# Layer B's output blocks and attention steps in another order

## The chip, the cores and the metric

The kernel runs on one core of a Trainium2 chip. The metric is the device time of one execution in microseconds (us), lower is better. The kernel before has a median of 1008.8 us over three runs (1007.71 to 1010.31).

Five engines matter: TensorE (PE in the profile) multiplies matrices, VectorE (DVE) and ScalarE (ACT) work on elements, GpSimd (POOL) issues some of the transfers, and SyncE (SP) issues the transfers of the weights. Each has its own list of instructions.

## The reference, cut to what matters

A trunk of two layers over 256 tokens of width 2048: layer A is a Mamba-2 mixer, layer B is attention over a window of 128 keys with one sink per head. Both end in a LayerNorm of `alpha * x + mixer(x)`. Layer B, which the change touches, computes:

```python
proj = x @ w_in                                # 2048 -> [q 2048 | gate 2048]
q = rope(proj[..., :2048] + q_bias)            # 32 heads of 64; 4 key groups of 8 heads
s = q . k * 64 ** -0.5                         # window of 128: masked elsewhere
m = max(max(s), sink);  p = exp(s - m)
p = p / (sum(p) + exp(sink - m))
o = (p @ v) * silu(gate)
x = layernorm(alpha * x + o @ w_out)
```

Keys and values are computed once, for 4 key groups, each shared by 8 query heads. The kernel handles one key group (512 columns of q, of the gate and of the input of `w_out`) at a time.

## The kernel before, in words

**Units of weights.** All weights stream through SBUF in units of 128 x 2048 numbers. `load_unit` (L120) fetches a unit in two halves of 512 KB from SyncE's queue into one of five raw buffers `wr`, and then splits each half into a high part `wh` (ScalarE, L133) and a low part `wl` (VectorE, L134), so that three matmuls of rounded operands give the product (`wh` and `wl` have four buffers each). `next_unit` (L179) keeps two units ahead of the one that TensorE works on.

**Layer B's blocks.** The work is a list of twelve blocks of four units each, `B_ORDER` (L39). For key group j:

- `q_block(j)` (L790): queries. Four units add into two PSUM tiles (one per half h of the 256 tokens), 24 matmuls of 512 columns a unit (L751 to L753). Then VectorE takes both tiles out of PSUM with the bias (L801), applies the rotary part (L739 to L744) and transposes 32 x 32 squares (`zq`, L806). GpSimd writes the result to DRAM (`qd`, L847) and reads it back turned (`qr`, L813); ScalarE scales it into `qT` (L817).
- `gate_block(j)` (L829): the gate, 48 matmuls of 256 columns a unit (L195 to L197), one PSUM tile a unit, then ScalarE and VectorE (L838, L839).
- `attend(j, h)` (L853): scores of one half (TensorE, L864), mask (L872, L873, L877), maximum (L881), exponentials (ScalarE, L887), division (L892). Then `turn_p` transposes into `z` (L898) and writes it to DRAM (`pd`, L847), `load_p` reads it back as `pT` (L905), `mask_p` makes a second, masked copy `pm` (L912, for h = 1 alone), and `pv` multiplies with the values (TensorE, L922) and with the gate, and splits the result into `oH` and `oL` (L929, L938, L939).
- an output block `("o", j)`: `out_unit` (L249) multiplies `oH`, `oL` with the units of `w_out`, 24 matmuls of 512 columns a unit (L255 to L257) into two PSUM tiles, one for each half; VectorE adds each to the residual `xr` (L264; L260 in the first block).

All matmuls of the blocks share four PSUM tiles `mm` (L81), the scores and values share another four, `ax` (L84). `z`, `zq`, `qr`, `p`, `pT` and `pm` share five buffers with the tag `pb`.

**Steps.** One unit is one step. After each unit `tick` (L204) counts down a list, `pending`; `later(n, fn)` (L201) puts a function on it that runs n steps on. So the attention of a key group is spread over the units of the blocks that follow its queries. Counted from the step T at which `q_block(j)` ends, before the change:

| what | step, j = 0 to 2 | step, j = 3 |
| --- | --- | --- |
| `load_q` (both halves) | T + 1 | T + 1 |
| `scale_q` (both halves) | T + 3 | T + 3 |
| `attend(j, 0)` | T + 4 | T + 4 |
| `attend(j, 1)` | T + 7 | T + 5 |
| `turn_p`, `load_p` of h = 0 | T + 6, T + 7 | T + 6, T + 7 |
| `turn_p`, `load_p` of h = 1 | T + 9, T + 10 | T + 7, T + 8 |
| `pv` of h = 0, of h = 1 | T + 10, T + 13 | T + 10, T + 11 |

With step 1 as the first unit of `("q", 0)`, the query blocks end at steps 4, 12, 20 and 32, and the output blocks start at steps 25, 33, 41 and 45.

**What sets the order.** The Python program is written in this order, and a planner then makes each engine's list from it when the kernel is built. It follows an estimate of its own of when each instruction's inputs are there; of those that are ready by that estimate, the one that was written earlier goes first. A step is thus an instruction's rank, not a fixed place: an instruction that the planner believes ready can stand ahead of ones written earlier whose inputs it expects later. What comes out is a fixed list for each engine, with waits; on the chip an instruction whose input is late holds up what stands behind it on its engine.

Of the kernel before, what the change touches and what calls it, by code (L numbers as in the profile page):

```python
# [35 lines left out]
BLOCKS = list(range(10))  # L36
BLOCKS0 = [6, 7, 8, 9, 0, 1, 2, 3, 4, 5]
CB_AT, ZT_AT, LD_AT, XD_AT, Y_AT, NSM = 4, 5, 6, 8, 9, 3
B_ORDER = [("q", 0), ("g", 0), ("q", 1), ("g", 1), ("q", 2), ("g", 2), ("o", 0), ("q", 3),  # L39
           ("o", 1), ("g", 3), ("o", 2), ("o", 3)]  # L40
ALPHA = (2.0 * 2) ** 0.25
NEG = -1.0e30
# [15 lines left out]
def trunk(ctx: ExitStack, tc: tile.TileContext, A: dict, out: bass.AP, dbg=None):  # L58
# [17 lines left out]
    def nm(s):  # L76
        uid[0] += 1
        return f"{s}_{uid[0]}"

    def mm_tile():  # L80
        return mm_ps.tile([P, 512], F32, tag="mm", name=nm("mm"), bufs=4)  # L81
# [89 lines left out]
    broken = set()  # L171
    for what, j in B_ORDER:
        if what == "g":
# [5 lines left out]
    def next_unit():  # L179
        if not units:  # L180
            units.extend(load_first())
            nc.sync.dma_start(pc[:], A["pc"])
        while len(units) < min(used[0] + 1 + AHEAD, len(srcs)):
            if len(units) == 5:
                nc.sync.dma_start(cc[:], A["cc"])
            if len(units) in (8, 9):
                i = len(units) - 8
                nc.sync.dma_start(xr[:, i, :], A["xk"][:, i, :])
                nc.scalar.activation(xr[:, i, :], xr[:, i, :], AF.Copy, scale=ALPHA)
            units.append(load_unit(srcs[len(units)], BROKEN if len(units) in broken else [WHOLE, WHOLE]))  # L190
        used[0] += 1
        return units[used[0] - 1]
# [8 lines left out]
    def later(n, fn):  # L201
        pending.append([n, fn])

    def tick():  # L204
        ready = []
        for it in list(pending):
            it[0] -= 1
            if it[0] <= 0:
                pending.remove(it)
                ready.append(it[1])  # L210
        for fn in ready:
            fn()
# [36 lines left out]
    def out_unit(aH, aL, h, u, nb, first, rms=None):  # L249

        ps = mm_tile()
        hs = slice(h * P, (h + 1) * P)
        for k in range(4):
            ks = slice(k * 512, (k + 1) * 512)
            nc.tensor.matmul(ps[:], aH[:, k, hs], u.h[:, ks], start=k == 0, stop=False)  # L255
            nc.tensor.matmul(ps[:], aL[:, k, hs], u.h[:, ks], start=False, stop=False)  # L256
            nc.tensor.matmul(ps[:], aH[:, k, hs], u.l[:, ks], start=False, stop=k == 3)  # L257
        v = xr[:, h, nb * 512 : (nb + 1) * 512]
        if first:
            nc.vector.scalar_tensor_tensor(v, v, ALPHA, ps[:], ALU.mult, ALU.add)  # L260
        elif rms is not None:
            nc.vector.scalar_tensor_tensor(v, ps[:], rms[:, h : h + 1], v, ALU.mult, ALU.add)
        else:
            nc.vector.tensor_tensor(v, v, ps[:], ALU.add)  # L264
# [462 lines left out]
    def bias_row(src):  # L727
        t = bp.tile([P, 512], F32, tag="bias", name=nm("bias"), bufs=2)
        nc.gpsimd.dma_start(t[:], src.partition_broadcast(P))
        return t  # L730

    def rope(v, h, n):

        c = cs[:, h : h + 1, :].to_broadcast([P, n, 8])
        s = sn[:, h : h + 1, :].to_broadcast([P, n, 8])
        t = bp.tile([P, 4, 8, 8], F32, tag="rt", name=nm("rt"), bufs=1)
        x1, x2 = v[:, :, 0:8], v[:, :, 8:16]
        a, b, d, e = [t[:, i, :n, :] for i in range(4)]
        nc.vector.tensor_tensor(a, x1, c, ALU.mult)  # L739
        nc.vector.tensor_tensor(b, x2, s, ALU.mult)  # L740
        nc.vector.tensor_tensor(d, x2, c, ALU.mult)
        nc.vector.tensor_tensor(e, x1, s, ALU.mult)
        nc.vector.tensor_tensor(x1, a, b, ALU.subtract)
        nc.vector.tensor_tensor(x2, d, e, ALU.add)  # L744

    def x_stat(ps, h, u, ui):
        for k in range(4):
            kk = ui * 4 + k
            ks = slice(k * 512, (k + 1) * 512)
            hs = slice(h * P, (h + 1) * P)  # L750
            nc.tensor.matmul(ps[:], x1H[:, kk, hs], u.h[:, ks], start=kk == 0, stop=False)  # L751
            nc.tensor.matmul(ps[:], x1L[:, kk, hs], u.h[:, ks], start=False, stop=False)  # L752
            nc.tensor.matmul(ps[:], x1H[:, kk, hs], u.l[:, ks], start=False, stop=kk == KT - 1)  # L753
# [36 lines left out]
    def q_block(j):  # L790
        pss = [mm_tile(), mm_tile()]
        qb = bias_row(A["qb"][j * 512 : (j + 1) * 512])
        for ui in range(4):
            u = next_unit()
            for h in range(2):
                x_stat(pss[h], h, u, ui)
            tick()
        for h in range(2):
            qt = bp.tile([P, 8, 64], F32, tag="qt", name=nm("qt"), bufs=2)
            qf = qt[:].rearrange("p a d -> p (a d)")  # L800
            nc.vector.tensor_tensor(qf, pss[h][:], qb[:], ALU.add)  # L801
            rope(qt[:], h, 8)

            def turn_q(h=h, qf=qf):
                z = bp.tile([P, 1024], F32, tag="pb", name=nm("zq"), bufs=5)[:, :512]
                nc.vector.transpose(  # L806
                    z.rearrange("p (c a t) -> p a c t", c=4, a=4), qf.rearrange("p (a c d) -> p a c d", a=4, c=4)
                )
                d = to_dram(z, 128, "qd")

                def load_q():
                    t = bp.tile([P, 8, 4, 32], F32, tag="pb", name=nm("qr"), bufs=5)[:, :4]
                    nc.gpsimd.dma_start(t.rearrange("p b a t -> p b (a t)"), d[:].rearrange("b p f -> p b f"))  # L813

                    def scale_q():
                        q2 = bp.tile([P, 4, P], F32, tag="qT", name=nm("qT"), bufs=2)
                        nc.scalar.activation(  # L817
                            q2[:].rearrange("p a (b t) -> p a b t", b=4), t.rearrange("p b a t -> p a b t"),
                            AF.Copy, scale=0.125,
                        )  # L820
                        qT[j, h] = q2

                    later(2, scale_q)

                later(1, load_q)

            turn_q()

    def gate_block(j):  # L829
        t = bp.tile([P, 4, S], F32, tag="sg", name=nm("sg"), bufs=2)  # L830
        sg[j] = t
        for p_ in range(4):
            u = next_unit()
            ps = mm_tile()
            for k in range(KT):
                mac(ps[:, :S], u.tile(0, k), u.tile(1, k), x1H[:, k, :], x1L[:, k, :], k == 0, k == KT - 1)
            tick()
            nc.scalar.activation(t[:, p_, :], ps[:, :S], AF.Tanh, scale=0.5)  # L838
            nc.vector.scalar_tensor_tensor(  # L839
                t[:, p_, :], t[:, p_, :], 1.0, ps[:, :S], ALU.add, ALU.mult  # L840
            )

    def to_dram(z, n, name):

        t = dram.tile([4, P, n], F32, tag=name, name=nm(name), bufs=2)
        for a in range(4):
            nc.gpsimd.dma_start(  # L847
                t[a, :, :].rearrange("(b t) f -> t b f", b=4),
                z[32 * a : 32 * a + 32, :].rearrange("p (b f) -> p b f", b=4),
            )  # L850
        return t

    def attend(j, h):  # L853
# [84 lines left out]
            nc.scalar.activation(oH[:, :, hs], o[:], AF.Copy)  # L938
            nc.vector.tensor_tensor(oL[:, :, hs], o[:], oH[:, :, hs].bitcast(F32), ALU.subtract)  # L939

        last = j == 3
        later(2, turn_p)
        later(3, load_p)
        later(5, mask_p)
        later(6, pv)
        if h == 0:
            later(1 if last else 3, lambda: attend(j, 1))

    for what, j in B_ORDER[:-1]:
        if what == "q":  # L950
            q_block(j)
            later(4, lambda j=j: attend(j, 0))
        elif what == "g":
            gate_block(j)
        else:
            for nb in range(4):
                u = next_unit()
                for h in range(2):
                    out_unit(*os_[j], h, u, nb, j == 0)
                tick()  # L960
# [140 lines left out]
```

## Time and profile before

| | |
| --- | --- |
| median of three runs | 1008.8 us (1007.71 to 1010.31) |
| the profiled execution | 1005.46 us |
| its span (first to last instruction) | 1003.6 us |
| PE busy | 983.6 us (98%) |
| DVE busy | 778.8 us (78%) |
| ACT busy | 559.3 us (56%) |
| POOL busy | 137.9 us (14%) |
| mean granted TensorE clock | 0.994 |
| first scores of layer B (L864) | 739.9 us from the span's start |
| last scores | 925.9 us |
| last values (L922) | 964.2 us |

PE's busy time counts an instruction from its start to a modelled end; matmuls overlap, so the pace of a stretch is read from the starts. The granted clock is a share of full speed. In a timeline or a group of instructions the bracket or the last column tells how long the engine stood idle before the instruction, and what ended that idle time.

### The profile page before, as it was taken

What the parts mean: (1) busy time and instruction counts of PE and PEld (TensorE: products, weight loads), DVE (VectorE), ACT (ScalarE), POOL (GpSimd) and SP (SyncE); (2) the same over time, 40 slices, a digit from 0 to 9 for tenths busy, and PEclk for the clock granted to TensorE, in tenths of its full rate; (3) what the DMA queues carried; (4) which work ended last, traced back from release to release, by engine and by line L of the source; (5) the groups of instructions that cost most, each with busy time, mean ns of one, the idle gap of its engine ahead of it and who ended that gap; (6) DMA issues with size and microseconds to landing.
All of it is one profiled execution on the core that took longest, in us unless ns stands there. A gap on an engine that the chain in (4) does not pass through costs nothing.

```text
span 1003.6 us, 17483 instructions
## 1 busy us (share of the span) xinstructions
PE 983.6 (98%) x6844; PEld 886.8 (88%) x6844; DVE 778.8 (78%) x1116; ACT 559.3 (56%) x928; POOL 137.9 (14%) x192
## 2 busy tenths in 40 slices
PE   7999999999999999999999999999999999998997
PEld 7999999999998998999999999877898888777965
DVE  6869997876797796796787687799658596966876
ACT  6585757637655665664664664445455464633632
POOL 0000303004003001200300300301204031110202
PEclk9999999999999999999999999999999999998998
DMA  8787686586677667667658458646757667566552
GB/s 314 273 276 258 199 277 230 164 286 168 210 232 222 216 203 244 205 190 254 200 174 278 143 195 272 231 133 224 237 184 243 229 214 248 191 226 209 185 216 85
DMA packets 69875, 219.24 MB, mean 218 GB/s; under 512 B 8144, under 2 KB 19680, under 8 KB 69024
## 3 DMA queue, kind: packets, MB, share of 16 engines
q1 hardware_dynamic: 64080, 199.48, 61.0%
q0 software_dynamic: 5424, 18.12, 5.2%
q8 instruction: 54, 0.88, 0.4%
q10 hardware_dynamic: 288, 0.52, 0.1%
q14 instruction: 29, 0.24, 0.1%
HBM read 205.90 MB, written 12.19 MB: 217 GB/s over the span
## 4 chain that ended last, share of the span: by engine, by line
PE 78%; DVE 7%; DMA 6%; ACT 4%; issue 3%; POOL 1%; SPq 0%; DVEq 0%; ACTq 0%; POOLq 0%
PE mm L195 15%; PE mm L196 15%; PE mm L197 15%; PE mm L255 7%; PE mm L256 6%; PE mm L257 6%; PE mm L751 3%; PE mm L752 3%; PE mm L753 3%; DVE wl L134 2%; PE ax L510 2%; ACT wh L133 2%; DMA wr<-in_wa 1%; PE ax L864 1%; PE ax L922 1%
## 5 line engine op out<-in xcount | busy, mean ns | idle before, releaser
L134 DVE TENSOR_TENSOR wl<-wr,wh 128x1024 fp32r<-128x1024 f32 (+2 forms) x342 | 397.4, 1180 | 114.1 <-ACT wh L133 112.7
L133 ACT ACTIVATE wh<-wr 128x1024 fp32r<-128x1024 f32 (+2 forms) x342 | 338.0, 1011 | 190.9 <-PE mm L196 68.1
L195 PE MATMUL mm<-xH,wh 128*128 128x256 f32 x1296 | 360.5, 278 | 6.2 <-ACT wh L153 5.5
L197 PE MATMUL mm<-xH,wl 128*128 128x256 f32 x1296 | 359.6, 278 | 1.9 <-DVE wl L134 1.9
L196 PE MATMUL mm<-xL,wh 128*128 128x256 f32 x1296 | 360.0, 278 | 0.0
L195 PEld LDWEIGHTS mm<-xH,wh 128*128 128x128 f32 x1296 | 244.5, 189 | 8.1 <-ACT wh L153 5.8
L197 PEld LDWEIGHTS mm<-xH,wl 128*128 128x128 f32 x1296 | 244.3, 189 | 2.6 <-DVE wl L134 2.6
L196 PEld LDWEIGHTS mm<-xL,wh 128*128 128x128 f32 x1296 | 244.5, 189 | 1.1
L526 POOL TENSOR_TENSOR yz<-yz,z 128x256 f32<-128x256 f32 x32 | 33.7, 1063 | 524.3 <-DVE yz L521 482.9
L255 PE MATMUL mm<-wh,yH 128*128 128x512 f32 x256 | 101.3, 396 | 0.0
L256 PE MATMUL mm<-wh,yL 128*128 128x512 f32 x256 | 99.9, 390 | 0.0
L257 PE MATMUL mm<-wl,yH 128*128 128x512 f32 x256 | 99.7, 389 | 0.0
L195 PE MATMUL mm<-x1H,wh 128*128 128x256 f32 x256 | 72.6, 284 | 3.0 <-DVE xr L264 3.0
L196 PE MATMUL mm<-x1L,wh 128*128 128x256 f32 x256 | 72.0, 281 | 0.0
L197 PE MATMUL mm<-x1H,wl 128*128 128x256 f32 x256 | 72.0, 281 | 0.0
L364 DVE SCALAR_TENSOR_TENSOR cv<-mm,pc,cv 128x255 f32<-128x255 f32 x144 | 68.7, 477 | 2.0 <-ACT cv L362 0.6
L751 PE MATMUL mm<-wh,x1H 128*128 128x512 f32 x160 | 63.5, 397 | 0.0
L753 PE MATMUL mm<-wl,x1H 128*128 128x512 f32 x160 | 62.7, 392 | 0.2 <-DVE wl L134 0.2
L752 PE MATMUL mm<-wh,x1L 128*128 128x512 f32 x160 | 62.6, 391 | 0.2 <-DVE x1L L715 0.2
L255 PEld LDWEIGHTS mm<-wh,yH 128*128 128x128 f32 x256 | 48.1, 188 | 10.7 <-DVE z L434 1.0
L257 PEld LDWEIGHTS mm<-wl,yH 128*128 128x128 f32 x256 | 48.1, 188 | 10.2
L256 PEld LDWEIGHTS mm<-wh,yL 128*128 128x128 f32 x256 | 48.1, 188 | 8.9
(188 smaller groups left out, 1317.0 us busy)
## 6 DMA issues: line engine op xcount, KB each, us to landing
wr<-in_wa SPq DMA_DIRECT2D x158, 512.0 KB, 5.3
wr<-in_wo SPq DMA_DIRECT2D x64, 512.0 KB, 4.9
wr<-in_wq SPq DMA_DIRECT2D x32, 512.0 KB, 5.0
wr<-in_wg SPq DMA_DIRECT2D x32, 512.0 KB, 5.4
wr<-in_wb SPq DMA_DIRECT2D x32, 512.0 KB, 6.5
rb<-rscr SPq DMA_DIRECT2D x16, 512.0 KB, 5.4
el<-rscr SPq DMA_DIRECT2D x16, 256.0 KB, 4.9
wr<-in_wkv SPq DMA_DIRECT2D x8, 512.0 KB, 5.0
```

Of the source, the lines that this page charges most:

```text
L133: nc.scalar.activation(h[:, sl], raw, AF.Copy)
L134: nc.vector.tensor_tensor(l[:, sl], raw, h[:, sl].bitcast(F32), ALU.subtract)
L195: nc.tensor.matmul(ps, ah, bh, start=first, stop=False)
L196: nc.tensor.matmul(ps, ah, bl, start=False, stop=False)
L197: nc.tensor.matmul(ps, al, bh, start=False, stop=last)
L255: nc.tensor.matmul(ps[:], aH[:, k, hs], u.h[:, ks], start=k == 0, stop=False)
L256: nc.tensor.matmul(ps[:], aL[:, k, hs], u.h[:, ks], start=False, stop=False)
L257: nc.tensor.matmul(ps[:], aH[:, k, hs], u.l[:, ks], start=False, stop=k == 3)
L364: nc.vector.scalar_tensor_tensor(a[:, sft:], ps[:, : S - sft], w(3 - sft), a[:, sft:], ALU.mult, ALU.add)
L751: nc.tensor.matmul(ps[:], x1H[:, kk, hs], u.h[:, ks], start=kk == 0, stop=False)
L752: nc.tensor.matmul(ps[:], x1L[:, kk, hs], u.h[:, ks], start=False, stop=False)
L753: nc.tensor.matmul(ps[:], x1H[:, kk, hs], u.l[:, ks], start=False, stop=kk == KT - 1)
```

## The change

Three things are altered. The block `("q", 3)` moves ahead of `("o", 0)`. `scale_q` comes four steps after `load_q` and not two, and the scores of h = 0 six steps after the end of the query block and not four, with those of h = 1 one step later for every key group (before: three steps for the first three, one for the last). And `mask_p` and `pv` come one step later after their scores (6 and 7, not 5 and 6).

```diff
-B_ORDER = [("q", 0), ("g", 0), ("q", 1), ("g", 1), ("q", 2), ("g", 2), ("o", 0), ("q", 3),
+B_ORDER = [("q", 0), ("g", 0), ("q", 1), ("g", 1), ("q", 2), ("g", 2), ("q", 3), ("o", 0),
            ("o", 1), ("g", 3), ("o", 2), ("o", 3)]
...
-                    later(2, scale_q)
+                    later(4, scale_q)
...
-        last = j == 3
         later(2, turn_p)
         later(3, load_p)
-        later(5, mask_p)
-        later(6, pv)
+        later(6, mask_p)
+        later(7, pv)
         if h == 0:
-            later(1 if last else 3, lambda: attend(j, 1))
+            later(1, lambda: attend(j, 1))
 
     for what, j in B_ORDER[:-1]:
         if what == "q":
             q_block(j)
-            later(4, lambda j=j: attend(j, 0))
+            later(6, lambda j=j: attend(j, 0))
```

After it, for every j: `scale_q` at T + 5, the scores at T + 6 and T + 7, `turn_p` at T + 8 and T + 9, `load_p` at T + 9 and T + 10, `mask_p` of h = 1 at T + 13, `pv` at T + 13 and T + 14. The query blocks end at steps 4, 12, 20 and 28; the first output block starts at step 29 and no longer at 25, the others at 33, 41 and 45 as before. No instruction is added or left out, and the streams of weights differ in order alone.

## The prediction

> **What bounds the kernel now.** The first view is the profile's page: TensorE is busy for nearly the whole span.
>
> ```profile
> PE 983.6 (98%) x6844; PEld 886.8 (88%) x6844; DVE 778.8 (78%) x1116; ACT 559.3 (56%) x928; POOL 137.9 (14%) x192
> ```
>
> No matmul is added or removed, so the change can move only time in which TensorE stands still or runs slowly inside layer B. The second view, what TensorE waited for from 640 us to the end, lists all of it (total us, times, longest):
>
> ```profile
> PE mm L195 <- DVE xr L264: 3.0, 1, 3.0
> ...
> PE ax L922 <- DMA pT<-pd: 0.9, 1, 0.9
> PE ax L922 <- DVE pm L912: 0.3, 1, 0.3
> ```
>
> The other rows of that answer belong to the seam before layer B and to the closing norm, which stay as they are. The third view, the stretches, shows what the long wait cost besides itself (columns: length, busy time and count of PE, PEld, DVE, ACT and POOL, granted clock, DMA share, GB/s):
>
> ```profile
> 914.35:917.34 2.99, 0.01 (x2) 0.00 (x1) 2.88 (x4) 2.99 (x6) 0.00 (x0) 0.88 0.21 49
> 917.34:923.26 5.92, 5.92 (x27) 5.92 (x28) 5.92 (x10) 2.12 (x4) 0.00 (x0) 0.50 0.89 290
> 923.26:925.85 2.59, 2.59 (x23) 2.46 (x22) 2.59 (x3) 0.00 (x0) 0.00 (x0) 0.97 0.78 291
> 839.70:913.20 73.50, 73.50 (x327) 56.22 (x326) 54.24 (x82) 32.07 (x67) 11.75 (x20) 1.00 0.61 202
> 960.00:966.00 6.00, 4.85 (x20) 2.41 (x19) 3.07 (x4) 1.69 (x2) 0.00 (x0) 1.00 0.87 360
> ```
>
> After 2.99 us of standing still the clock is 0.50 for 5.92 us: 27 matmuls there, 23 in the next 2.59 us. At full clock the work of those 5.92 us takes 2.96, so the place costs 2.99 + 2.96 = **5.95 us**. The second place, 962 to 965 us, is 6.00 - 4.85 = **1.15 us** and its clock stays 1.00. Together 7.1 us: the most that this change can win.
>
> What caused the first? The fourth view, the chain of waits, names the steps (start, length, work):
>
> ```profile
> 913.04 0.24 PE mm L257
> 913.29 1.14 ACT wh L133 x2
> 914.49 0.93 issue
> 915.47 1.01 DVE wl L134
> 916.60 0.69 DVE xr L264
> 917.34 0.58 PE mm L195
> ```
>
> TensorE began the last gate block only when a residual add (L264) had given back a PSUM tile; that add stood behind weight splits on VectorE, and these waited for ScalarE. ScalarE's timeline says why it was late (the bracket is idle time before the row):
>
> ```profile
> 910.32 0.63 ACT L817 ACTIVATE qT<-qr 128x512 f32<-128x512 f32 x1 [5.28 <-DMA qr<-qd]
> 912.76 0.63 ACT L817 ACTIVATE qT<-qr 128x512 f32<-128x512 f32 x1 [1.80 <-DMA qr<-qd]
> 913.29 5.11 ACT L133 ACTIVATE wh<-wr 128x128 fp32r<-128x128 f32 x8
> ```
>
> The scaling of the fourth group's queries waited 5.28 + 1.80 us for a transfer, and eight pieces of split stood behind it, ready, for they then ran without a gap. VectorE paid in turn, and had been late already, since a mask had held it until 891 us:
>
> ```profile
> 891.08 1.23 DVE L912 TENSOR_TENSOR pm<-pT,cc 128x1024 f32<-128x1024 f32 x1 [8.07 <-issue]
> ...
> 913.62 0.29 DVE L134 TENSOR_TENSOR wl<-wr,wh 128x128 fp32r<-128x128 f32 x1 [6.32 <-ACT wh L133]
> ```
>
> **The change part by part.** One step is one unit: the third and fourth unit of the second output block start 907.66 - 902.12 = 5.54 us apart.
>
> ```profile
> 902.12 0.47 PE L255 MATMUL mm<-wh,oH 128*128 128x512 f32 x1
> ...
> 907.66 0.39 PE L255 MATMUL mm<-wh,oH 128*128 128x512 f32 x1
> ```
>
> *Queries scaled at T + 5, scores at T + 6.* When are the queries there after the change? Every query block but the first will end one step after the scores of h = 1 of the group before, as the second and third do now. The chain of waits and ScalarE's timeline give both:
>
> ```profile
> 757.58 1.93 PE ax L864 x16
> ...
> 808.04 1.93 PE ax L864 x16
> ```
> ```profile
> 783.37 0.63 ACT L817 ACTIVATE qT<-qr 128x512 f32<-128x512 f32 x1 [4.49 <-DMA qr<-qd]
> ...
> 836.80 0.63 ACT L817 ACTIVATE qT<-qr 128x512 f32<-128x512 f32 x1 [6.79 <-DMA qr<-qd]
> ```
>
> The blocks end at 757.58 + 1.93 + 5.54 = 765.1 and 815.5 us, so the first half of the queries is there 18.3 and 21.3 us, 3.3 and 3.8 steps, later. Six steps (33 us) cover that with 12 us to spare; four steps (22 us) had about 1. So no scores wait. What ScalarE holds up is decided by rank: at T + 3 the scaling was written ahead of the splits fetched in the fourth unit after the query block, at T + 5 it is written behind them and behind the next ones. Where the planner sees both ready, the split now goes first, and the 6.32 us on VectorE are no longer ahead of residual adds. I count the whole 5.95 us as gone. From the other side, if the planner still expects `qr` before the split, nothing of it goes (first rival).
>
> *Last group's attention.* Its query block ends at step 28 and not 32, its values come at steps 41 and 42 and not 42 and 43, and between its scores of h = 1 (step 35, not 37) and their values lie seven steps and not six. Two steps more, some 11 us, stand against a wait of 1.15: it goes. If the cover failed, those 1.15 us would come back.
>
> *Values at seven steps.* `pv` of the other groups waits for nothing now, so this wins nothing; it moves the masks, whose wait on VectorE (8.07 us above) is free where TensorE works on gates or queries and not where output units need their PSUM tiles back.
>
> *Two output blocks in a row.* Here the change can lose. Steps 25 to 36 are one output, one query and one output block before (the stretch from 839.70 to 913.20 above, VectorE busy 54.24 of 73.50 us), and one query and two output blocks after. The groups of VectorE's instructions in layer B give what comes in (last columns: busy, mean ns | idle before, releaser):
>
> ```profile
> L134 DVE TENSOR_TENSOR wl<-wr,wh 128x1024 fp32r<-128x1024 f32 x69 | 82.8, 1217 | 14.7 <-ACT wh L133 14.6
> L264 DVE TENSOR_TENSOR xr<-xr,mm 128x512 f32<-128x512 f32 x16 | 10.3, 679 | 0.0
> L892 DVE TENSOR_TENSOR p<-p,sm 128x1024 f32<-128x1024 f32 x8 | 9.8, 1222 | 0.1
> L881 DVE TENSOR_REDUCE sm<-p 128x8 f32<-128x1024 f32 x8 | 9.7, 1216 | 0.1
> L873 DVE COPY_PREDICATED p<-cc,ax 128x256 f32<-128x256 int32 x16 | 5.8, 438 | 0.0
> L929 DVE SCALAR_TENSOR_TENSOR o<-ax,sg 128x512 f32<-128x512 f32 x8 | 5.5, 687 | 1.3 <-PE ax L922 1.3
> L939 DVE TENSOR_TENSOR oL<-o,oH 128x512 fp32r<-128x512 f32 x8 | 5.5, 686 | 0.0
> L877 DVE TENSOR_TENSOR p<-ax,cc 128x512 f32<-128x512 f32 x8 | 5.1, 683 | 0.0
> L912 DVE TENSOR_TENSOR pm<-pT,cc 128x1024 f32<-128x1024 f32 x4 | 4.9, 1226 | 22.0 <-DMA pT<-pd 13.9 <-issue 8.1
> L890 DVE TENSOR_TENSOR sm<-sm 128x8 f32<-128x8 f32 x8 | 1.3, 161 | 15.5 <-ACT p L887 15.5
> ```
>
> Both halves of the last group's scores move in (steps 34 and 35, before 36 and 37), and so does one `pv`. The first half: two L877, one L881, one L892 and five small operations like L890 = 1.37 + 1.22 + 1.22 + 0.81 = 4.6 us; the second has four L873 in place of L877, 5.0; a `pv` is 0.69 + 0.69 = 1.4. So VectorE has 54.2 + 11.0 = 65.2 us of work. TensorE's own 73.5 grow by two more scores (1.93 for h = 1; about 1.1 for each h = 0, half the columns, one of which moved in from step 24) and a `pv` of about 1.0, to 78.6 us. Between lie 13.4 us of room, and VectorE's waits fill them: each of four halves waits for exponentials 15.5 / 7 = 2.2 us, 8.9 together, and the mask up to 8.1. Sum 82.2, over by 3.6; without the mask's wait under by 4.5. A residual add may be late by about a step (an output unit takes two of four tiles), 5.5 us, which absorbs the 3.6 on average but not each bunch: right after the third query block two attention halves, the drain of the queries and the first residual adds meet. I take **1.0 us** of new standing still, nearer to none because VectorE also has no 8 us behind it when that block ends. The bounds are 0 and what the slower rival gives.
>
> *Buffers and GpSimd.* The reads of `pT` now stand near the writes of `qd` on GpSimd's list and can hold them; the 12 us of spare time at the scores cover one such wait. The five `pb` buffers are just enough at step T + 9. Both: nothing, at worst within the last rival.
>
> The sum: 1005.46 (profiled execution: its span of 1003.6 and 1.9 around it) - 5.95 - 1.15 + 1.0 = 999.4 us, that is -6.1. The median of the runs is 3.3 us above that execution; carried over, 1008.8 - 6.1 = **1002.7 us**.
>
> [...]
>
> **The rivals.**
>
> *The stall only moves.* The planner ranks by its estimate of when `qr` lands. All three ScalarE rows above show it early by 4.5 to 6.8 us, so it may still place the scaling ahead of a split two steps before it was written. The first output block then takes the stall that the second has now, at the same 5.95; only the 1.15 are won: 1007.6. Against it: a query block now ends with scores of h = 1 in VectorE's list, which delays `qr` in the planner's estimate too, past the next free split buffer. That the change doesn't do what it says (the lists hardly differ, for rank isn't place) ends at the same number or at 1008.8.
>
> *VectorE becomes the bound in the two output blocks.* Place: steps 29 to 36. It decides once VectorE's waits there exceed 78.6 + 5.5 - 65.2 = 18.9 us. If the mask waits its 8.1, the exponentials 8.9 and the split again 6.3 for ScalarE, they are 23.3: TensorE stands 4.4 us, in two or three pieces behind late adds. Two that draw the clock down cost 2 x 2.96 more, 10.3 in all against 7.1 won: +3.2, or 1012.0. For it: 22.0 us of waits at L912 in four times. Against it: a busy list leaves the planner no idle time into which it would pull a mask.
>
> **How the numbers follow.** Forecast 0.53; stall moves or nothing changes 0.30; VectorE bound 0.17. A measurement of this kernel tells about 0.3% (3.0 us) from no change. Forecast alone: 1000 (everything won, and 1.3 us of the runs' scatter) to 1005. The range for all reaches into the slower rival: 1000 to 1011. Faster by over 0.3% is the forecast and a few cases in which the moved stall is small: 0.55; within 0.3%: 0.29; slower: 0.16.
>
> **What would show it.** Right: no wait of TensorE over 1 us between 700 and 990 us, granted clock 1.00 throughout that stretch, the `qT` rows of the last group with no idle run of splits behind them, and no wait of L922 on `pT`. The first rival: a wait of a matmul on L260 or L264 near the end of the first output block, behind `qT` and splits. The second: several waits on L260 and L264 in steps 29 to 36 with VectorE busy above 85% there. Wrong altogether: new waits of L864 on `qT` or of DVE rows on `pd` or `qd` for a `pb` buffer.

## The result, and the profile after

The changed kernel takes **1001.54 us** (median of 4 runs, 1001.36 to 1003.57); the kernel before, run beside it, 1008.62 us (4 runs, 1007.71 to 1010.31). The ratio is **0.9932, 95% interval 0.9914 to 0.9951**: 7.1 us faster by the medians. The profiled execution took 1001.62 us, 3.84 us less than the one of before (1005.46).

The page of the kernel after, its span and busy time:

```profile
span 999.8 us, 17489 instructions
...
PE 981.3 (98%) x6844; PEld 883.5 (88%) x6844; DVE 777.3 (78%) x1116; ACT 558.8 (56%) x928; POOL 138.1 (14%) x192
```

What TensorE waited for in the kernel after, from 640 us to the end (total us, times, longest). The rows left out belong to the seam ahead of layer B and to the closing norm:

```profile
PE mm L255 <- DVE sg L839: 0.8, 1, 0.8
PE ax L864 <- DVE p L877: 0.7, 1, 0.7
```

The 3.0 us in front of the last gate block and both waits of the values (0.9 and 0.3) are gone; two shorter waits, on other lines, are new. The stretches of the kernel after that hold the two (length, busy time and count of PE, granted clock, DMA share, GB/s):

```profile
910.00:920.00 10.00, 9.28 (x47) 1.00 0.39 128
...
950.00:960.00 10.00, 9.17 (x39) 1.00 0.83 296
```

The clock stays at 1.00, where before it was 0.50 for 5.92 us. ScalarE's timeline of the kernel after shows that the scaling's waits went too (the bracket is idle time before the row):

```profile
892.89 1.06 ACT L133 ACTIVATE wh<-wr 128x1024 fp32r<-128x1024 f32 x1 [3.10 <-DMA wr<-in_wb]
893.86 0.61 ACT L817 ACTIVATE qT<-qr 128x512 f32<-128x512 f32 x1
895.61 1.06 ACT L133 ACTIVATE wh<-wr 128x1024 fp32r<-128x1024 f32 x1 [1.15 <-DMA wr<-in_wb]
896.58 0.61 ACT L817 ACTIVATE qT<-qr 128x512 f32<-128x512 f32 x1
```

The last group's two scalings carry no bracket: each runs right behind a split, its queries already there. Before, they had waited 5.28 and 1.80 us with ready splits behind them.

Where do the new waits come from? VectorE's timeline of the kernel after holds all four masked copies, and what stands behind the last:

```profile
797.60 1.23 DVE L912 TENSOR_TENSOR pm<-pT,cc 128x1024 f32<-128x1024 f32 x1 [7.86 <-DMA pT<-pd]
...
848.87 1.23 DVE L912 TENSOR_TENSOR pm<-pT,cc 128x1024 f32<-128x1024 f32 x1 [9.22 <-DMA pT<-pd]
...
899.92 1.22 DVE L912 TENSOR_TENSOR pm<-pT,cc 128x1024 f32<-128x1024 f32 x1 [1.99 <-DMA pT<-pd]
...
949.12 1.23 DVE L912 TENSOR_TENSOR pm<-pT,cc 128x1024 f32<-128x1024 f32 x1 [5.99 <-DMA pT<-pd]
950.27 1.22 DVE L134 TENSOR_TENSOR wl<-wr,wh 128x1024 fp32r<-128x1024 f32 x1
951.40 0.41 DVE L839 SCALAR_TENSOR_TENSOR sg<-sg,mm 128x256 f32<-128x256 f32 x1
```

They waited 25.1 us for the read of `pT` (22.0 before). Behind the last stood a weight split and then the drain of the last gate unit (L839: VectorE takes the product out of PSUM), which gives back a PSUM tile that the output block after it needs. TensorE's timeline of the kernel after:

```profile
912.40 0.70 PE L864 MATMUL ax<-kT,qT 64*128 64x256 f32 x2 [0.72 <-DVE p L877]
...
951.87 0.50 PE L255 MATMUL mm<-wh,oH 128*128 128x512 f32 x1 [0.83 <-DVE sg L839]
```

The other place is the score tiles. The matmuls of h = 1 (64x256, 64 of them) in the kernel before and, in the second fence, after (busy, mean ns | idle before):

```profile
L864 PE MATMUL ax<-kT,qT 64*128 64x256 f32 x64 | 8.0, 389 | 0.0
```
```profile
L864 PE MATMUL ax<-kT,qT 64*128 64x256 f32 x64 | 9.8, 400 | 0.8 <-DVE p L877 0.7
```

That is 9.8 + 0.8 - 8.0 = 2.6 us more for the same matmuls. With the gate's drain, 951.87 - 950.65 less one matmul's 0.23 us, or 1.0 (the last matmul ahead of the wait started at 950.65), the change stands for **3.6 us** in new places. 7.1 won less 3.6 is 3.5. From the first matmul of layer B's projections (L751) to the last of its output (L257), TensorE's timelines give 992.34 - 668.28 = 324.06 us before and 989.29 - 669.29 = 320.00 after: 4.06 less, of which I do not assign 0.6. That the whole profiles differ by a like number, 3.84, is chance: layer A, which the change doesn't touch, ended 1.0 us later in the profile of after, and what follows the last output matmul was 0.8 us shorter.

### The profile page after: what moved, and what is told of

Same layout as the page of the kernel before. It is cut to its first block, busy times and chain, and to the rows that moved or that the text cites. A ratio compares the mean times of both kernels' runs of the same rounds, so it can differ in the third digit from the quotient of the medians.

```text
span 999.8 us, 17489 instructions
## 1 busy us (share of the span) xinstructions
PE 981.3 (98%) x6844; PEld 883.5 (88%) x6844; DVE 777.3 (78%) x1116; ACT 558.8 (56%) x928; POOL 138.1 (14%) x192
## 4 chain that ended last, share of the span: by engine, by line
PE 70%; DVE 12%; DMA 7%; ACT 5%; issue 4%; POOL 1%; SPq 0%; DVEq 0%; ACTq 0%; POOLq 0%
PE mm L195 13%; PE mm L196 13%; PE mm L197 13%; PE mm L255 6%; PE mm L256 6%; PE mm L257 6%; DVE wl L134 4%; PE mm L751 3%; PE mm L752 3%; PE mm L753 3%; DMA pT<-pd 2%; PE ax L510 2%; ACT wh L133 2%; DMA wr<-in_wa 1%; ACT e L403 1%
## 5 line engine op out<-in xcount | busy, mean ns | idle before, releaser
L195 PE MATMUL mm<-xH,wh 128*128 128x256 f32 x1296 | 360.4, 278 | 7.2 <-ACT wh L153 6.2
L195 PEld LDWEIGHTS mm<-xH,wh 128*128 128x128 f32 x1296 | 244.4, 189 | 8.9 <-ACT wh L153 6.5
L257 PE MATMUL mm<-wl,yH 128*128 128x512 f32 x256 | 99.7, 389 | 0.0
L195 PE MATMUL mm<-x1H,wh 128*128 128x256 f32 x256 | 70.7, 276 | 0.0
L751 PE MATMUL mm<-wh,x1H 128*128 128x512 f32 x160 | 63.7, 398 | 0.0
L257 PEld LDWEIGHTS mm<-wl,yH 128*128 128x128 f32 x256 | 48.1, 188 | 10.2
```

What stands on the lines that cost most here:

```text
L195: nc.tensor.matmul(ps, ah, bh, start=first, stop=False)
```

## The experiments

B is the kernel before, A the changed kernel. Ratios are to B, run beside each of them.

### The kernel before once more

No edit.

> The kernel before, unchanged, beside itself. All theories: a ratio of 1.000 within its interval. What it is to tell: the profiled execution of before took 1005.46 us, its timed runs 1008.6, and the change won 7.1 us in the runs but only 3.8 us between the two profiles. Theory: the stall in front of the last gate block differs in length from execution to execution (2.98 us standing and 2.96 us of slow clock in the one profile shown), so a second profile shows another length there and the same elsewhere; in an execution of 1008 to 1009 us it would be 5 to 6 us standing, or a second place. Rival: the 3 us lie outside layer B, and layer B is the same within 0.3 us.

1007.68 us (12 runs, 1004.04 to 1010.42), ratio 1.0005 [0.9988, 1.0022]. The profiled execution took 1007.6 us, and its waits of TensorE are not those of the first profile:

```profile
PE mm L195 <- DVE xr L264: 4.2, 1, 4.2
...
PE mm L255 <- DVE xr L264: 1.1, 1, 1.1
PE ax L922 <- DMA pT<-pd: 1.0, 1, 1.0
PE mm L255 <- DVE qt L801: 0.9, 1, 0.9
...
PE ax L922 <- DVE pm L912: 0.3, 1, 0.3
```

The same chain, but longer: 4.2 us where the first profile had 3.0, and two more waits of about 1 us. The transfer that ScalarE waits for lands later; its second scaling in this execution of B:

```profile
915.95 0.63 ACT L817 ACTIVATE qT<-qr 128x512 f32<-128x512 f32 x1 [3.02 <-DMA qr<-qd]
916.48 5.10 ACT L133 ACTIVATE wh<-wr 128x128 fp32r<-128x128 f32 x8
```

The bracket was 1.80 in the first profile. So B's loss differs between executions, 7.5 us of these waits here against 4.2 there, and from the first L751 to the last L257 it took 995.18 - 668.23 = 326.95 us, 2.9 more than in the first profile. That is one reason why the medians can differ by 7.1 us where the two profiles differ by 3.84: the prediction sized the gain by one of B's better executions. Layer A, the same in all these kernels, adds its own scatter: the first L751 starts between 667.40 and 671.16 us in the fourteen profiles.

### One link of the chain cut: the last group's scaling on GpSimd

```diff
-                        nc.scalar.activation(qo, qi, AF.Copy, scale=0.125)
+                        if j == 3:
+                            nc.gpsimd.tensor_scalar(qo, qi, 0.125, None, ALU.mult)
+                        else:
+                            nc.scalar.activation(qo, qi, AF.Copy, scale=0.125)
```

(on B; `qo` and `qi` are the two views of L817)

> The kernel before, with one edit: for the last key group alone the scaling of the queries (two instructions, L817) runs on GpSimd and not on ScalarE; no other instruction changes its engine or its place. Theory (the stall before the last gate block comes from ScalarE standing at this scaling, with splits behind it and residual adds behind those): the wait of L195 on L264 and the slow clock behind it are gone, the time falls by about 6 us, to 1002.7 (ratio 0.994). The last values still wait 1.15 us. Rival (VectorE was late anyway, from the mask's 8.07 us): TensorE still stands 2 to 3 us there, the time stays within 2 us of 1008.6.

1000.65 us (6 runs, 1000.30 to 1002.86), ratio **0.9937 [0.9918, 0.9957]**. What TensorE still waited for in layer B of this kernel (L865 is B's L864, shifted by the edit; the new L819 is the scaling on GpSimd):

```profile
PE ax L865 <- POOL qT L819: 0.8, 1, 0.8
```

Two instructions put on another engine, and the order of blocks and every step as before, win what the whole change wins. On the four engines VectorE, ScalarE, GpSimd and SyncE no other instruction of layer B changed its place. ScalarE's wait for the queries was a link of the stall, as the prediction said.

### Another link: the third group's mask on GpSimd

```diff
-                nc.vector.tensor_tensor(
+                (nc.gpsimd if j == 2 else nc.vector).tensor_tensor(
                     m[:], t[:],
```

(on B, L912)

> The kernel before, with one edit: the masked copy of the third key group (one instruction, L912) runs on GpSimd and not on VectorE; nothing else moves. Theory (the mask's wait of 8.07 us at 883 to 891 us delays the last query block's drain, so its transfers, so the scaling on ScalarE): the last group's zq, qr and qT come 6 to 8 us earlier, the stall before the last gate block is gone; the copy itself takes 4 us there and may hold the third group's last values up by 1 us; about 1003.5 us (ratio 0.995). Rival (the scaling's wait stands by itself, whatever VectorE does before): the stall stays, 1008 to 1009.

1002.09 us (8 runs, 998.94 to 1005.37), ratio **0.9947 [0.9926, 0.9968]**. In this kernel ScalarE's timeline is as bad as B's:

```profile
908.08 0.63 ACT L817 ACTIVATE qT<-qr 128x512 f32<-128x512 f32 x1 [3.30 <-DMA qr<-qd]
908.62 4.08 ACT L133 ACTIVATE wh<-wr 128x128 fp32r<-128x128 f32 x6
```

and yet nothing of TensorE waits on L264; its one wait of layer B is the last values':

```profile
PE ax L922 <- DMA pT<-pd: 2.6, 1, 2.6
```

So B's stall needed both: the mask's 8 us on VectorE and then the scaling's 7 on ScalarE. Either alone is absorbed. (The copy took 2.41 us on GpSimd; the 4 that I had expected was an estimate, and no run showed it.)

### The step of the scaling

```diff
-                    later(4, scale_q)
+                    later(2, scale_q)
```

(on A)

> The change, with the queries scaled at T + 3 again and not at T + 5. The prediction's theory (the step of the scaling is its rank, and the rank is what puts it behind the weight splits): the scaling of the last group goes ahead of splits again, ScalarE holds them up, VectorE's splits and residual adds are late and TensorE stalls in an output block; a wait on L260 or L264 of 2 us or more, and 1005 to 1008 us, ratio 0.997 to 1.000. The rival (the planner places the scaling by its own estimate of when the transfer lands, which the step does not move; what moved it is the query block's place and the attention written ahead of it): the lists differ in next to nothing from those of the change, no such wait, 1000 to 1003 us, ratio 0.991 to 0.995. I expect the rival.

1002.57 us (10 runs, 999.81 to 1003.96), ratio 0.9949 [0.993, 0.9968]; A's own is 0.9932 and, once more, 0.993. On all five engines the lists are A's but for two neighbouring rows of ScalarE that changed places. ScalarE's timeline for the last group:

```profile
895.03 1.06 ACT L133 ACTIVATE wh<-wr 128x1024 fp32r<-128x1024 f32 x1 [5.33 <-DMA wr<-in_wb]
896.00 0.61 ACT L817 ACTIVATE qT<-qr 128x512 f32<-128x512 f32 x1
```

Written two steps earlier, the scaling still stands behind the splits and waits for nothing. The prediction's "decided by rank" falls. That the planner puts this instruction by its estimate of when `qr` lands fits, but is not shown.

### Order and steps apart

Old order of blocks, all the new steps:

```diff
-B_ORDER = [..., ("g", 2), ("q", 3), ("o", 0),
+B_ORDER = [..., ("g", 2), ("o", 0), ("q", 3),
```

(on A)

> All new steps in the old order of blocks. Theory (the new steps need the query block moved ahead): the stall before the last gate block goes, 6 us won, but the last scores come at steps 38 and 39 and the last values only when the list is drained behind step 44; with five steps between, not six, and 1.15 us already short at six, TensorE stands 6 to 8 us in front of the last output block and 3 us more go to the slow clock: 1008 to 1014 us, a wait of L922 on pT or pm of 6 us or more. Rival (the later steps alone carry the gain): 1002 us.

1016.07 us (9 runs, 1013.07 to 1017.88), ratio **1.0077 [1.0054, 1.0099]**: slower than B by 0.8%, a little beyond what I had expected. TensorE's two waits, in its timeline:

```profile
853.31 0.80 PE L255 MATMUL mm<-wh,oH 128*128 128x512 f32 x1 [5.05 <-DVE sg L839]
...
974.59 1.98 PE L922 MATMUL ax<-pT,vt 128*64 128x512 f32 x4 [5.30 <-DMA pT<-pd]
```

The second is the last group's: with its query block at the old place, the new steps put its values at steps 45 and 46, where the last output block begins. The first is the gate's drain once more, at the other place where an output block follows a gate block; VectorE's timeline there:

```profile
850.56 1.23 DVE L912 TENSOR_TENSOR pm<-pT,cc 128x1024 f32<-128x1024 f32 x1 [9.16 <-DMA pT<-pd]
851.70 1.22 DVE L134 TENSOR_TENSOR wl<-wr,wh 128x1024 fp32r<-128x1024 f32 x1
852.84 0.41 DVE L839 SCALAR_TENSOR_TENSOR sg<-sg,mm 128x256 f32<-128x256 f32 x1
```

Old order, the new steps for the first three groups alone:

```diff
-                    later(2, scale_q)
+                    later(2 if j == 3 else 4, scale_q)
...
-        later(5, mask_p)
-        later(6, pv)
+        later(5 if last else 6, mask_p)
+        later(6 if last else 7, pv)
...
-            later(1 if last else 3, lambda: attend(j, 1))
+            later(1, lambda: attend(j, 1))
...
-            later(4, lambda j=j: attend(j, 0))
+            later(4 if j == 3 else 6, lambda j=j: attend(j, 0))
```

(on B)

> The order of blocks before, with the new steps for the first three groups and the old ones for the last: the half of the change that the best form so far leaves out. Theory (the early groups' new steps win nothing by themselves: their scores and values waited for nothing before, and with the two halves of scores in neighbouring steps VectorE reads the score tiles late): the stall in front of the last gate block stays, or is shorter only by what the third mask's wait gives, and score tiles lose 1 to 3 us; 1006 to 1011 us, ratio 0.998 to 1.003. Rival (the third mask's wait of 8 to 10 us was the first link of the stall, so one step more for it takes the stall away): 1000 to 1003, ratio 0.992 to 0.995.

1004.74 us (10 runs, 1002.76 to 1007.50), ratio 0.9977 [0.9956, 0.9998]: neither of my two numbers. The profile explains the middle. The third mask no longer waits, and though the last scaling still waits 5.95 us with splits behind it, the stall at L195 is gone: the rival's mechanism. But the gate's drain takes 2.22 us at 850 us and the last values 2.40 at 962, the second with a slow clock behind it (0.59 and 0.55 in the two stretches of 2 us that follow).

New order, the new steps for the last group alone, those of B for the other three:

```diff
-                    later(2, scale_q)
+                    later(4 if j == 3 else 2, scale_q)
...
-        later(5, mask_p)
-        later(6, pv)
+        later(6 if last else 5, mask_p)
+        later(7 if last else 6, pv)
...
-            later(4, lambda j=j: attend(j, 0))
+            later(6 if j == 3 else 4, lambda j=j: attend(j, 0))
```

(on B, with A's `B_ORDER`)

> The new order of blocks, and the new steps for the last key group alone; groups 0 to 2 keep the steps of before (scaling at T + 3, scores at T + 4 and T + 7, values six steps after the scores). Theory (the gain comes from moving the last query block ahead, so that neither its queries nor its last values are late; the steps of the other groups win nothing and cost the waits of scores for a PSUM tile, 0.15 and 0.95 us at the second and third group): no slower than the change, 1000 to 1002 us. Rival (the steps of all groups carry the gain): 1005 to 1008, with waits between 760 and 900 us that the change doesn't have.

999.05 us (6 runs, 998.54 to 1000.99), ratio **0.992 [0.9901, 0.994]**. The same kernel a second time:

> The new order with the new steps for the last key group alone, once more, beside the change on one chip. Theory (the new steps of groups 0 to 2 win nothing and cost the waits for PSUM tiles): 2 us below the change, a ratio to before of 0.991. Rival (the difference seen so far is that of two chips): equal to the change within 0.5 us.

1000.2 us (6 runs, 998.48 to 1002.97), ratio 0.9917 [0.9887, 0.9948]. And the change itself a second time, beside it:

> The changed kernel, unchanged, as a measure on the same chip as the three others of this call. All theories: a ratio to before of 0.993, and waits of the scores for a PSUM tile of about 0.7 us and of an output block for the last gate of about 0.8 us in the profile.

1001.65 us (8 runs, 999.94 to 1003.76), ratio 0.993 [0.9904, 0.9957]. The reorder with the last group's steps carries the whole gain. The early groups' new steps add nothing to it and may cost 1 to 2.5 us; the intervals overlap, so that is not shown.

ScalarE's timeline of the kernel without the early groups' new steps (its first profile) says something about the cause that the change's own profile hides:

```profile
878.49 0.63 ACT L817 ACTIVATE qT<-qr 128x512 f32<-128x512 f32 x1 [4.28 <-DMA qr<-qd]
879.03 1.99 ACT L133 ACTIVATE wh<-wr 128x1024 fp32r<-128x1024 f32 x2
...
888.86 0.63 ACT L817 ACTIVATE qT<-qr 128x512 f32<-128x512 f32 x1 [2.03 <-DMA qr<-qd]
```

The last group's scaling waits 4.28 and 2.03 us again (4.41 and 1.24 in the second profile), with ready splits behind the first half, in the first output block; the mask behind it waits 7.02 us; and no matmul of an output or gate block waits. So the gain doesn't need the scaling behind the splits. Why this order absorbs these waits, where the old one stalled, is open.

In its second profile the change waits at the gate's drain for 1.6 us and for a residual add (L260) for 1.5, with the score tiles at 8.2 us and no idle time: about the same loss as in the first (3.3 us), spread otherwise. The form without the early steps has a single wait worth naming, in its two executions:

```profile
895.72 1.08 PE L922 MATMUL ax<-pT,vt 128*64 128x512 f32 x4 [0.47 <-DMA pT<-pd]
```
```profile
894.90 1.08 PE L922 MATMUL ax<-pT,vt 128*64 128x512 f32 x4 [1.20 <-DMA pT<-pd]
```

The new order with all the old steps was not tried.

### Two attempts at what is left that missed

The scores of h = 1 two steps after those of h = 0, to give VectorE time to empty the score tiles:

```diff
-            later(1, lambda: attend(j, 1))
+            later(2, lambda: attend(j, 1))
```

(on A)

> The change with one number altered: the scores of h = 1 come two steps after those of h = 0 and not one, for all key groups. Theory (what the change still loses is that the second scores find their PSUM tiles not yet read by VectorE, 0.15, 0.95 and 1.6 us at groups 1 to 3 by the starts of TensorE's instructions): these waits go, about 2 us below the change, 0.991 to before; the last values come at step 43 and still stand free. Rival (TensorE waits because VectorE has too much to do in these steps altogether): the waits move to residual adds or values and the time stays that of the change.

1010.59 us (12 runs, 1008.14 to 1015.49), ratio **1.0028 [1.0008, 1.0049]**, where I had expected a gain. The score tiles are relieved (8.0 us, no idle time), but the attention of h = 1 moves a step on, its mask with it, and VectorE now stands 9.26 us at the last mask, ahead of the gate's drain (VectorE's timeline, then TensorE's):

```profile
961.23 1.22 DVE L912 TENSOR_TENSOR pm<-pT,cc 128x1024 f32<-128x1024 f32 x1 [9.26 <-issue]
962.38 0.41 DVE L839 SCALAR_TENSOR_TENSOR sg<-sg,mm 128x256 f32<-128x256 f32 x1
```
```profile
962.84 0.79 PE L255 MATMUL mm<-wh,oH 128*128 128x512 f32 x1 [4.81 <-DVE sg L839]
```

TensorE stood 4.81 us for it, and 4.5 us more in three waits on residual adds (L260, L264). The score tiles gave back 2.6 us at most; the gate's drain behind the mask alone cost more.

The last group's mask and values one step later, on the form with the new order and the last group's steps:

```diff
-        later(6 if last else 5, mask_p)
-        later(7 if last else 6, pv)
+        later(7 if last else 5, mask_p)
+        later(8 if last else 6, pv)
```

> The kernel with the new order, the new steps for the last group alone and the old ones for the first three, and now with the last group's mask at seven steps and its values at eight after their scores (six and seven in the first form). Theory (what that form leaves, 0.7 to 1.4 us of waits on pT and pm, is a step too few for the last values): the wait goes, and the time is 0.7 to 1.4 us lower: 998 to 999.5, ratio 0.990 to 0.991. Rival (the wait only moves, to the first units of the third output block, whose products of oH then come late behind the values, or to the mask's place on VectorE's list): 999 to 1000.5 as in the first form, ratio 0.9915 to 0.9925, with a wait on oH, sg or xr in place of that on pT.

999.95 us (8 runs, 996.86 to 1002.40), ratio 0.993 [0.9906, 0.9953]: no gain over 0.992 and 0.9917. Its premise was mine and wrong: the wait at 895 us shown above is that of the third group's values, since the last group's scores follow only at 903 and 910 us; the edit doesn't touch it. In this execution it happened to be nil, and 1.0 us came up at the gate's drain, behind the last mask.

### All masks off VectorE

```diff
-                nc.vector.tensor_tensor(
+                (nc.gpsimd).tensor_tensor(
                     m[:], t[:],
```

(on A, L912)

> The change, with the masked copy (L912) of all four groups on GpSimd in place of VectorE. Theory (what the change leaves is VectorE held at a mask that waits for its DRAM read, ahead of the gate's drain and of residual adds): the waits of TensorE on sg (L839, 0.8 to 1.6 us) and on xr (L260, 1.5 us) go, VectorE's waits at L912 of 25 us with them, and the time falls by 1 to 2.5 us to 999 to 1000.5, ratio 0.990 to 0.992. Rival (GpSimd's copy takes some 4 us and holds its own list, so the writes and reads of qd and pd come later and scores or values wait): the same 1001 to 1002 as the change or above, with a new wait on pT, pm or qT. Of the last values, which follow the mask by one step of 5.5 us, I expect a wait of at most 1 us.

**998.07 us** (6 runs, 996.33 to 999.26), ratio **0.9911 [0.988, 0.9942]**, the lowest time of all. Beside it ran the kernel with the change's lists (the scaling's step, above), 999.81 to 1003.96 us in ten runs: no run of the one reaches those of the other. GpSimd's group, which carries the wait now, and the scores' group of this kernel:

```profile
L912 POOL TENSOR_TENSOR pm<-pT,cc 128x1024 f32<-128x1024 f32 x4 | 11.0, 2758 | 26.1 <-DMA pT<-pd 26.1
...
L864 PE MATMUL ax<-kT,qT 64*128 64x256 f32 x64 | 8.0, 389 | 0.0
```

A copy takes 2.76 us and not 1.23, and the wait for `pT` is as long as ever (26.1 us), but nothing that empties PSUM stands behind it. TensorE's waits of layer B are all gone, at the gate's drain and at the residual adds, and the scores are back at 8.0 us. From the first L751 to the last L257 it took 315.91 us, against 320.00 and 319.63 in the two profiles of the change. So the waits at the gate's drain and at the residual adds come from the masks' wait on VectorE. For the score tiles this is likely but not shown, since the change's second profile has 8.2 us there with the masks on VectorE.

## Why the prediction was right or wrong

**The total was right; two terms behind it were not, and they have opposite signs.** 1002.7 was forecast and 1001.54 measured; that it came so near is in part luck.

- **What can be won, 7.1 us.** Right for the profiled execution: 5.95 and 1.15 are both gone. As the most that the change can win it was wrong, for B loses more in other executions. The step "carried over, 1008.8 - 6.1" let one execution stand for all. Between the two profiles the change won 3.84, between the medians 7.1. That B's other executions lie above the first by longer waits of this kind is shown for one of them.
- **The chain.** Right for the stall before, with both links shown: take away the scaling's wait or the mask's, and the stall is gone. The prediction put the scaling first and the mask as what "had been late already"; neither does it alone.
- **"What ScalarE holds up is decided by rank."** Wrong. With the scaling written at T + 3 again the lists are the change's but for one pair. The first rival's words "rank isn't place" were right, but its time wasn't, for the stall went all the same. Nor does the reorder alone put the scaling behind the splits: with the early groups' old steps it stands ahead of them again and waits 4.28 and 2.03 us. The reason given against that rival (scores of h = 1 now stand ahead of the query block's end on VectorE's list, so the planner expects `qr` later) fits both kernels, but is argued and not shown.
- **"... if the planner still expects `qr` before the split, nothing of it goes".** Wrong, and with it the first rival's price of 5.95 us moved into the first output block: the same kernel with the early groups' old steps is in that case and takes 999.05 and 1000.2 us. That the 5.95 us would go was right, but the scaling's new place, which the prediction gave as the reason, was not needed for it.
- **Six steps cover the queries.** Right: `qT` was written at 897 us and the scores came at 904, and no L864 waits on it.
- **Last values, 1.15 us.** Right: no wait at L922.
- **Values at seven steps "wins nothing".** Its side effect was named and not priced: a mask's wait is free "where TensorE works on gates or queries and not where output units need their PSUM tiles back". The last mask waited from 943 to 949 us, in an output block that had begun at 941.45, and the tile that was missing was the last gate unit's (1.0 us here, 5.05 with the old order). Nor need a query block be safe: of the score tiles' 2.6 us some 1.0 fell at 859 us, in the last query block, 10 us behind a mask that had waited 9.22. That this mask was the cause is likely, not shown.
- **New standing, 1.0 us.** This term was mis-sized: 3.6 in the first profile and 3.3 in the second, mostly at tiles that the step didn't name. Residual adds, which it named, show only in the change's second profile (1.5 us).
- **Buffers and GpSimd: nothing.** Right: no wait on `pb`, `pd` or `qd` in TensorE's answer.
- **"VectorE becomes the bound."** Not in the change. But its mechanism, a mask's wait that fills VectorE's slack until TensorE stands and the clock drops, is what makes one neighbour of the change slower than before (1.0028: the mask waits 9.26 us, TensorE stands 4.81, and the clock is 0.66 from 960 to 970 us), and a part of what slows another (1.0077), whose last values also wait 5.30 us for a read. The change sits one step from it.
- **What would show it.** No wait over 1 us and a clock of 1.00 held in the first profile; in the second the waits were 1.6 and 1.5 us, and the time was the same.

## What to carry to other kernels

An instruction that waits for a DRAM round trip shouldn't stand on the list of an engine that empties PSUM: moving four masked copies to an engine busy for 14% of the span, each 2.2 times as long there, took every wait of TensorE in layer B away. Where a planner makes the lists, read them before crediting a step with a place; a step may move nothing. And profile the kernel before twice before sizing a gain by its waits: here they were 4.2 us in one execution and 7.5 in the other.

## What the runs showed of the hardware

The clock dropped behind gaps of TensorE shorter than the 2.99 us of the kernel before, and not behind each. Stretches right behind a gap of 2.14 us (the kernel with h = 1 two steps on; length, PE busy and count, clock, DMA share, GB/s):

```profile
910.18:912.32 2.14, 0.00 (x1) 1.00 0.00 0
912.32:914.32 2.00, 2.00 (x6) 0.63 0.00 0
914.32:916.32 2.00, 2.00 (x7) 0.52 0.56 119
916.32:918.32 2.00, 2.00 (x11) 1.00 0.83 234
```

and, in the kernel with the early steps in the old order, behind one of 2.22 us, which ended at 850.47, and one of 2.40, which ended at 961.91:

```profile
852.00:854.00 2.00, 2.00 (x11) 1.00 0.82 234
...
962.00:964.00 2.00, 2.00 (x6) 0.59 0.96 403
964.00:966.00 2.00, 2.00 (x6) 0.55 0.41 154
```

The gap of 2.14 us cost (0.37 + 0.48) / 0.50 x 2.00 = 3.4 us at half pace, that of 2.22 nothing (the clock is 1.00 over the whole of 850 to 860 us), that of 2.40 again 3.4. In the same way, the kernel before had 6.8 us of half clock from 910 to 930 us (0.83 in both stretches of 10 us), and that with all new steps in the old order 10.2 from 970 to 990 (0.66 and 0.83), where TensorE had stood 5.30. Behind the waits of 0.72 and 0.83 us in the change's first profile and of 1.59 in its second the clock stayed 1.00. In the closing norm of the first, behind four matmuls of a single row and a gap of 0.89 us, it was 0.72 from 993.5 to 994 us and 0.50 in the microsecond after. So the length of a gap didn't settle it alone in these runs; what else did is not shown.

The four reads of `pT`, 512 KB each, left VectorE waiting between 1.99 and 9.22 us within one execution of the change.
